# Scores by compressed and by selected keys in one matmul, and 32 units of attention in place of 48

## The chip, the cores and the metric

The kernel runs on one core of one Trainium2 chip. The metric is the device time of one execution in microseconds. The core has five engines with queues of their own: TensorE (PE in the profile; PEld is its weight load), VectorE (DVE), ScalarE (ACT), GpSimd (POOL) and SyncE (SP), which issues the transfers. TensorE multiplies a stationary 128-row operand with a moving one of up to 512 columns and writes into PSUM, eight banks of 512 columns each; DVE and ACT read them out.

## What is computed

One layer of a decoder for a prompt of 1024 tokens and eight single-token samples. The part that the change touches is the attention of the prompt, with eight heads in two groups of four, head width 64:

```python
def nsa_attend(q, gates, qpos, kc, vc, ksb, vsb, ovl, kw, vw, kwpos):
    s = einsum('bqghd,bcgd->bghqc', q, kc) * scale           # 63 compressed keys
    p_cmp = masked_softmax(s, c_end <= qpos)
    o_cmp = einsum('bghqc,bcgd->bqghd', p_cmp, vc)
    ...                                                       # top 16 of 16 blocks: all selected
    p = masked_softmax(q . kg * scale, kpos <= qpos)          # selected keys
    o_sel = p . vg
    p = masked_softmax(q . kw * scale, (dt >= 0) & (dt < 512))   # sliding window
    o_win = p . vw
    return gates[..., 0:1] * o_cmp + gates[..., 1:2] * o_sel + gates[..., 2:3] * o_win
```

Around it stand a norm with conditioning, one wide projection `z = h @ w_in`, a short gated convolution as a second branch, and three output projections.

## The kernel before

Values are kept in 32 bits, and each product is made of a high and a low half of its operands: a projection is three matmuls for each 128-deep slice (`Hh` by `wh`, `Hl` by `wh`, `Hh` by `wl`), a score two (`qh` and `ql`, lines 937 to 974). The attention runs after the key and value projections, over eight blocks of 128 queries.

**Units.** `unit(i, g, br)` (line 914) is the work of query block `i`, group `g` and branch `br`: 0 compressed (64 key columns), 1 selected (128 to 1024 columns, all blocks up to `i`), 2 window (128 to 640). Keys are cut into chunks of at most 512 columns by `chunks` (line 889). There are 48 units, in the order block, group, branch (line 1021).

**Two halves of a unit.** `a_steps` (line 937) goes over four heads `j`. For each chunk it makes two matmuls into a PSUM bank of tag `S` (three banks), then one pass on DVE that adds the mask, writes the scores to SBUF tile `P` and keeps their running minimum in `mx` (line 953; scores are negated). After a head's last chunk ACT takes the exponential with its sum (line 956). After the fourth head DVE makes reciprocals and multiplies in the gate (lines 960 to 962), and the weights are scaled: on DVE for three heads (line 969), on ACT for the last where rows are longer than 256 (line 967), on POOL for the compressed branch, one instruction for each head (line 971). `b_steps` (line 977) turns the weights, 128 keys at a time: four transposes on PE into a bank of tag `T` (two banks), a copy on ACT for the high half (`ph`), a subtraction on DVE for the low half (`pl`), and two matmuls with the values into the one bank of tag `O`, which collects all three branches of a block and group. For the compressed branch it is four transposes from 64 columns, one operand `pc` that holds both halves, and one matmul that opens bank `O`. After the window branch ACT and DVE write the result to `QO` (line 1017).

**Laying over each other.** The loop from line 1037 emits the first half of unit `n` with the second half of unit `n - LAG`, `LAG` being 2, alternating in proportion to their counts of steps. After each step `advance` (line 1028) emits some of the filler: 288 steps of three matmuls each from the projections of the convolution branch (`fill_gen`, line 883), paced by a listed time `est` for each unit, at least 4.0 us. `prep_q` (line 902) makes the halves of a block's queries on ACT, DVE and POOL before its first unit. Weights for the filler come by transfers on SP, are rounded on ACT and subtracted on POOL (`W.lo, W.hi = P, A`). The order of emission is a priority: a scheduler places the instructions in the queues when the program is built, by its own estimates of readiness, and each queue then runs in order. Tiles of one tag share a fixed number of buffers (`bufs`); `P0`, `P1` and `P2` have one each.

**Key tiles.** `make_keys` (line 604) writes the high and low half of the keys into `KS[b][g]`, 128 rows by 1024 columns (line 755); `kc` holds the compressed keys in the same form, 64 columns for each group. What the filler leaves, and the fourth part of the convolution, follow after the attention on the same engines.

Of the kernel before, what the change touches and what calls it, by code (L numbers as in the profile page):

```python
# [19 lines left out]
F32 = mybir.dt.float32  # L20
F32R = mybir.dt.float32r
# [64 lines left out]
def _build(ctx, tc, nc, I, O):  # L86
# [27 lines left out]
    def sub(eng, out, a, b):  # L114
        eng.tensor_tensor(out=out, in0=a, in1=b, op=OP.subtract)  # L115
# [636 lines left out]
    run(proj(q_evac(3)), {(1, 4): lambda: compress2(1)})  # L752
    xctx.close()
    kp = pool("kp", "right", att)
    KS = [[kp.tile([128, T], F32R, name=f"K{b}{g}") for g in range(2)] for b in range(2)]
# [130 lines left out]

    W.lo, W.hi = P, A

    def chunks(n):
        if n <= 512:  # L890
            return [n]
        return {640: [384, 256], 768: [512, 256], 896: [512, 384], 1024: [512, 512]}[n]

    class Unit:
        pass

# [12 lines left out]
            sub(P, QL[g][r], QO[r, :, qs], hh[g][r])  # L909
        QT[i] = hh  # L910

    WMAX = {0: 64, 1: 1024, 2: 640}

    def unit(i, g, br):
        u = Unit()
        u.i, u.g, u.br = i, g, br
        if br == 0:
            u.blocks, u.n = [0], 64
            u.ch = [(0, 64, cmsk[:, 56 - 8 * i:120 - 8 * i])]
        else:  # L920
            b0 = 0 if br == 1 else max(0, i - 4)
            u.blocks = list(range(b0, i + 1))
            u.n = 128 * len(u.blocks)
            edge = br == 2 and i >= 4
            u.ch, o = [], 0
            cl = chunks(u.n)
            for ci, n in enumerate(cl):
                m = msk[:, 128:128 + n]
                if ci == len(cl) - 1:
                    m = msk[:, 768 - n:768]  # L930
                elif ci == 0 and edge:
                    m = msk[:, 0:n]
                u.ch.append((o, n, m))
                o += n
        return u

    def a_steps(u):
        u.P = ap.tile([128, 4, WMAX[u.br]], F32, name=f"P{u.br}", tag=f"P{u.br}", bufs=1)
        u.mx = ap.tile([128, 4, 2], F32, name="mx", tag="mx", bufs=3)
        u.sm = ap.tile([128, 8], F32, name="sm", tag="sm", bufs=3)  # L940
        if u.br == 0:
            K = kc[:, u.g, :]
        else:
            K = KS[u.br - 1][u.g]
        k0 = u.blocks[0] * 128
        for j in range(4):
            hh = QT[u.i]
            for ci, (o, n, m) in enumerate(u.ch):
                ps = bank("S")
                mm(ps[:, :n], hh[u.g][:, j, :], K[:, k0 + o:k0 + o + n], True, False)  # L950
                mm(ps[:, :n], QL[u.g][:, j, :], K[:, k0 + o:k0 + o + n], False, True)
                init = 0.1 * BIG if ci == 0 else u.mx[:, j, ci - 1:ci]
                V.tensor_tensor_reduce(out=u.P[:, j, o:o + n], in0=ps[:, :n], in1=m, scale=1.0, scalar=init,  # L953
                                       op0=OP.add, op1=OP.min, accum_out=u.mx[:, j, ci:ci + 1])
                if ci == len(u.ch) - 1:
                    A.activation(u.P[:, j, 0:u.n], u.P[:, j, 0:u.n], AF.Exp, bias=u.mx[:, j, ci:ci + 1], scale=-1.0,  # L956
                                 accum_out=u.sm[:, j:j + 1])
                    if j == 3:
                        if u.br == 0:
                            V.tensor_scalar(u.sm[:, 0:4], u.sm[:, 0:4], 1e-30, None, op0=OP.max)  # L960
                        V.reciprocal(u.sm[:, 4:8], u.sm[:, 0:4])
                        V.tensor_tensor(out=u.sm[:, 4:8], in0=u.sm[:, 4:8],  # L962
                                        in1=gate[:, u.i, 12 * u.g + u.br:12 * u.g + u.br + 10:3], op=OP.mult)
                        for jj in range(4):
                            p = u.P[:, jj, 0:u.n]
                            if u.br > 0 and (jj == 3 and u.n > 256):
                                A.activation(p, p, AF.Copy, scale=u.sm[:, 4 + jj:5 + jj])
                            elif u.br > 0:
                                V.tensor_scalar(p, p, u.sm[:, 4 + jj:5 + jj], None, op0=OP.mult)  # L969
                            else:  # L970
                                P.tensor_tensor(out=p, in0=p, in1=u.sm[:, 4 + jj:5 + jj].to_broadcast([128, u.n]),
                                                op=OP.mult)
                yield max(0.2, 2 * n * 0.00042)

    OB = {}

    def b_steps(u):
        key = (u.i, u.g)
        if u.br == 0:
# [11 lines left out]
        pend = []  # L991

        def pv(kb, ph, pl, last):
            v = VS[u.br - 1]
            mm(OB[key], v[:, kb, u.g, :], pl, False, False)
            mm(OB[key], v[:, kb, u.g, :], ph, False, last)

        for n, kb in enumerate(u.blocks):
            pt = bank("T")
            for j in range(4):  # L1000
                PE.transpose(pt[:, j * 128:(j + 1) * 128], u.P[:, j, n * 128:(n + 1) * 128], ident)  # L1001
# [4 lines left out]
            pend.append((kb, ph, pl))  # L1006
            if len(pend) > 2:
                pv(*pend.pop(0), False)
            yield 0.87
# [12 lines left out]
    filler = fill_gen()  # L1022
    state = {"t": 0.0, "f": 0.0}
    est = lambda u: max(4.0, sum(2 * n * 0.00042 for _, n, _ in u.ch) * 4 + 0.87 * len(u.blocks))
    total = sum(est(u) for u in units)
    NFILL = 3 * 4 * 24

    def advance(dt):
        state["t"] += dt
        while filler and state["f"] < NFILL * min(1.0, state["t"] / total) - 1e-6:  # L1030
            state["f"] += 1
            next(filler, None)

    LAG = 2
    prep_q(0)
    done_q = 0
    for n in range(len(units) + LAG):
        la = []
        if n < len(units):
            u = units[n]  # L1040
            if u.i > done_q:
                prep_q(u.i)
                done_q = u.i
            la = a_steps(units[n])
        lb = b_steps(units[n - LAG]) if n >= LAG else iter(())

        na = 4 * len(units[n].ch) if n < len(units) else 0
        nb = len(units[n - LAG].blocks) + 1 if n >= LAG else 0
        ia = ib = 0
        share = est(units[min(n, len(units) - 1)]) / max(1, na + nb)  # L1050
        if n == len(units):
            share = 0
        while ia < na or ib < nb:
            if ib >= nb or (ia < na and ia * nb <= ib * na):
                next(la)
                ia += 1
            else:
                next(lb)
                ib += 1
            advance(share)  # L1060
        for _ in lb:
            pass
        for _ in la:
            pass
    for _ in filler:
        pass
# [362 lines left out]
```

## Time and profile before

| | us |
|---|---|
| median of 3 runs | 1097.35 |
| lowest and highest | 1094.35, 1097.61 |
| the profiled execution | 1093.98 |
| its span, first to last instruction | 1092.2 |
| PE busy | 1051.6 |
| DVE busy | 669.5 |
| ACT busy | 453.4 |
| POOL busy | 113.5 |

All rows come from the profiled execution; its span is 1.8 us shorter than its time. An instruction's busy time runs from its start to its end. On PE the end is modelled and matmuls overlap, so what a matmul costs is read from the distance to the start of the next. "Idle before" is time for which the engine stood still ahead of an instruction, with the engine and the output that released it. The attention stage lies from the first compressed score at 231.5 us to about 603 us; ahead of it are the norm, the projections of queries, keys and values and the compression, behind it projections that keep PE busy almost without a break.

### The profile page before, as it was taken

What the parts mean: (1) busy time and instruction counts of PE and PEld (TensorE: products, weight loads), DVE (VectorE), ACT (ScalarE), POOL (GpSimd) and SP (SyncE); (2) the same over time, 40 slices, a digit from 0 to 9 for tenths busy, and PEclk for the clock granted to TensorE, in tenths of its full rate; (3) what the DMA queues carried; (4) which work ended last, traced back from release to release, by engine and by line L of the source; (5) the groups of instructions that cost most, each with busy time, mean ns of one, the idle gap of its engine ahead of it and who ended that gap; (6) DMA issues with size and microseconds to landing.
All of it is one profiled execution on the core that took longest, in us unless ns stands there. A gap on an engine that the chain in (4) does not pass through costs nothing.

```text
span 1092.2 us, 17219 instructions
## 1 busy us (share of the span) xinstructions
PE 1051.6 (96%) x6406; PEld 967.0 (89%) x6406; DVE 669.5 (61%) x1789; ACT 453.4 (42%) x1006; POOL 113.5 (10%) x154
## 2 busy tenths in 40 slices
PE   5898999999999999999999999999999999999997
PEld 4688999988888899889888999999999999998785
DVE  4676656458987898879878734434455321584433
ACT  5566533356777777766666111111012111121221
POOL 3100000113222121211111010000000000020000
PEclk8899999989999999999999999999999999999999
DMA  9752242200000000000000412442232121332222
GB/s 324 212 147 75 77 101 59 76 23 21 19 20 21 20 20 20 20 20 9 13 20 23 116 40 69 131 148 69 76 75 53 39 59 39 99 114 79 78 78 77
DMA packets 103407, 75.97 MB, mean 70 GB/s; under 512 B 23873, under 2 KB 92680, under 8 KB 103324
## 3 DMA queue, kind: packets, MB, share of 16 engines
q1 hardware_dynamic: 103324, 74.88, 24.1%
q8 instruction: 50, 0.82, 0.3%
q14 instruction: 33, 0.27, 0.1%
HBM read 65.85 MB, written 9.01 MB: 69 GB/s over the span
## 4 chain that ended last, share of the span: by engine, by line
PE 79%; DVE 12%; ACT 4%; issue 1%; DMA 1%; SPq 0%; DVEq 0%; POOLq 0%; ACTq 0%; POOL 0%
PE psacc L106 47%; PE psS L106 18%; PE psO L106 6%; PE psT L1001 5%; DVE P L969 3%; DVE P L953 2%; ACT P L956 1%; DVE pl L115 1%; PE psT L106 1%; DVE pc L115 1%; DVE qh L112 1%; ACT xf L110 1%; DVE sm L962 1%; DVE QO L1017 1%; PE psT L357 1%
## 5 line engine op out<-in xcount | busy, mean ns | idle before, releaser
L106 PE MATMUL psacc<-Hh,wh 128*128 128x344 f32 x1072 | 356.6, 333 | 3.7 <-DVE Hh L112 3.7
L106 PE MATMUL psacc<-Hh,wl 128*128 128x344 f32 x1072 | 345.5, 323 | 1.0 <-DVE wl L115 1.0
L106 PE MATMUL psacc<-Hl,wh 128*128 128x344 f32 x1072 | 345.2, 322 | 0.0
L106 PEld LDWEIGHTS psacc<-Hh,wh 128*128 128x128 f32 x1072 | 203.2, 190 | 11.9 <-DVE Hh L112 4.2
L106 PEld LDWEIGHTS psacc<-Hl,wh 128*128 128x128 f32 x1072 | 203.1, 189 | 5.2 <-DVE Hl L115 0.5
L106 PEld LDWEIGHTS psacc<-Hh,wl 128*128 128x128 f32 x1072 | 203.0, 189 | 3.6 <-DVE wl L115 1.8
L956 ACT ACTIVATE P<-P,mx 128x64 f32<-128x64 f32 (+8 forms) x192 | 115.2, 601 | 48.5 <-DVE mx L953 47.8
L112 DVE CAST wh<-wraw 128x512 fp32r<-128x512 f32 x78 | 34.0, 442 | 121.0 <-PE psacc L106 114.5
L115 DVE TENSOR_TENSOR pl<-psT,ph 128x512 fp32r<-128x512 f32 x132 | 89.7, 687 | 26.7 <-ACT ph L110 26.1
L115 DVE TENSOR_TENSOR wl<-wraw,wh 128x512 fp32r<-128x512 f32 x112 | 76.5, 687 | 29.0 <-ACT wh L110 24.7
L110 ACT ACTIVATE ph<-psT 128x512 fp32r<-128x512 f32 x132 | 77.3, 590 | 36.9 <-PE psT L1001 36.5
L953 DVE CUSTOM_DVE_ANT_0 P<-psS,kbig 128x64 f32<-128x64 f32 (+4 forms) x192 | 81.3, 434 | 11.0 <-PE psS L106 9.9
L1001 PE MATMUL psT<-ident,P 128*128 128x128 f32 x528 | 82.6, 275 | 2.7 <-DVE mx L953 1.4
L1001 PEld LDWEIGHTS psT<-ident,P 128*128 128x128 f32 x528 | 63.6, 140 | 13.5 <-issue 3.3
L106 PE MATMUL psS<-K,qh 128*128 128x384 f32 (+3 forms) x192 | 66.2, 347 | 1.9 <-DVE mx L953 1.6
L115 POOL TENSOR_TENSOR wl<-wraw,wh 128x512 fp32r<-128x512 f32 x28 | 37.2, 1327 | 269.5 <-ACT wh L110 268.8
L106 PE MATMUL psS<-K,ql 128*128 128x384 f32 (+3 forms) x192 | 64.0, 335 | 0.0
L106 PE MATMUL psO<-pl,V 128*128 128x512 f32 x132 | 60.1, 456 | 1.0 <-DVE pl L115 0.9
L110 ACT ACTIVATE wh<-wraw 128x512 fp32r<-128x512 f32 x62 | 38.9, 628 | 41.6 <-PE psS L106 20.3
L106 PE MATMUL psO<-ph,V 128*128 128x512 f32 x132 | 52.1, 395 | 0.0
L969 DVE TENSOR_SCALAR P<-P,sm 128x640 f32<-128x640 f32 (+7 forms) x104 | 47.3, 513 | 0.7
L1220 ACT ACTIVATE M<-psacc 128x344 f32<-128x344 f32 x24 | 11.0, 457 | 87.8 <-PE psacc L106 87.8
(347 smaller groups left out, 1794.8 us busy)
## 6 DMA issues: line engine op xcount, KB each, us to landing
wraw<-w_in SPq DMA_DIRECT2D x76, 256.0 KB
x<-x_prompt SPq DMA_DIRECT2D x8, 512.0 KB
x<-w_ada SPq DMA_DIRECT2D x16, 256.0 KB
ar<-w_ada SPq DMA_DIRECT2D x16, 256.0 KB
wraw<-w_in SPq DMA_DIRECT2D x32, 128.0 KB
wraw<-w_cmp SPq DMA_DIRECT2D x16, 256.0 KB
wraw<-w_ada SPq DMA_DIRECT2D x16, 256.0 KB
wor<-w_out SPq DMA_DIRECT2D x16, 256.0 KB
```

Source lines behind the costliest of these rows:

```text
L106: PE.matmul(out, lhsT, rhs, start=start, stop=stop, skip_group_check=True)
L110: A.activation(out, in_, AF.Copy)
L112: eng.tensor_copy(out, in_)
L115: eng.tensor_tensor(out=out, in0=a, in1=b, op=OP.subtract)
L357: PE.matmul(ps[o:o + 32, :], cf[:, k, :], wraw.pop((b, k)), start=k < 4, stop=k >= 4, skip_group_check=True, tile_position=(0, o))
L953: V.tensor_tensor_reduce(out=u.P[:, j, o:o + n], in0=ps[:, :n], in1=m, scale=1.0, scalar=init, op0=OP.add, op1=OP.min, accum_out=u.mx[:, j ...
L956: A.activation(u.P[:, j, 0:u.n], u.P[:, j, 0:u.n], AF.Exp, bias=u.mx[:, j, ci:ci + 1], scale=-1.0, accum_out=u.sm[:, j:j + 1])
L962: V.tensor_tensor(out=u.sm[:, 4:8], in0=u.sm[:, 4:8], in1=gate[:, u.i, 12 * u.g + u.br:12 * u.g + u.br + 10:3], op=OP.mult)
L969: V.tensor_scalar(p, p, u.sm[:, 4 + jj:5 + jj], None, op0=OP.mult)
L1001: PE.transpose(pt[:, j * 128:(j + 1) * 128], u.P[:, j, n * 128:(n + 1) * 128], ident)
L1017: V.tensor_tensor(out=QO[r, :, 128 * u.i:128 * u.i + 128], in0=o[0:64].rearrange("p (j q) -> p j q", j=4), in1=tmp, op=OP.add)
L1220: A.activation(M[:, f, cs], acc, AF.Tanh, scale=0.5)
```

## The change

The compressed branch is no unit any more. The tile of the selected keys is widened by 64 columns in front, into which the compressed keys are copied, and the first chunk of a selected unit is scored together with them: one matmul over 64 + n columns, then two passes on DVE, one for each part, into `P0` and `P1` with minima and sums of their own. Chunks of selected keys are cut anew so that 64 more columns fit into a bank. POOL scales all four heads of the compressed weights in one instruction. The second half of a selected unit begins with the transposes of the compressed weights; their product with the values is emitted after the transposes of the first block of keys. There are 32 units. The second half of unit `n - 1` is laid beside the first half of unit `n`: steps of both get places on a line from 0 to 1 by listed times, the second half from `w` on, which stands for 2.5 us; the filler is emitted along the same line.

```diff
-            copy(A, KS[b][g][r, :], raw[r, 0:T])
-            sub(V, KS[b][g][o, :], raw[r, 0:T], KS[b][g][r, :])
+            ks = slice(KC[b], KC[b] + T)
+            copy(A, KS[b][g][r, ks], raw[r, 0:T])
+            sub(V, KS[b][g][o, ks], raw[r, 0:T], KS[b][g][r, ks])
...
+    KC = [64, 0]
+    KS = [[kp.tile([128, KC[b] + T], F32R, name=f"K{b}{g}") for g in range(2)] for b in range(2)]
+    for g in range(2):
+        copy(V, KS[0][g][:, 0:64], kc[:, g, :])
...
-        return {640: [384, 256], 768: [512, 256], 896: [512, 384], 1024: [512, 512]}[n]
+    CHUNKS = {1: {128: [128], 256: [256], 384: [384], 512: [256, 256], 640: [384, 256], 768: [384, 384],
+                  896: [448, 448], 1024: [384, 320, 320]},
+              2: {128: [128], 256: [256], 384: [384], 512: [512], 640: [384, 256]}}
...
+            subs = [(len(u.parts) - 1, o, n, m)]
+            k0 = KC[br - 1] + 128 * b0 + o
+            if ci == 0 and br == 1:
+                subs.insert(0, (0, 0, 64, cmsk[:, 56 - 8 * i:120 - 8 * i]))
+                k0 = 0
+            u.ch.append((k0, sum(x[2] for x in subs), subs))
...
+            for k0, nt, subs in u.ch:
                 ps = bank("S")
+                mm(ps[:, :nt], hh[u.g][:, j, :], K[:, k0:k0 + nt], True, False)
+                mm(ps[:, :nt], QL[u.g][:, j, :], K[:, k0:k0 + nt], False, True)
+                c0 = 0
+                for x, o, n, m in subs:
...
+                    V.tensor_tensor_reduce(out=Pb[:, j, o:o + n], in0=ps[:, c0:c0 + n], in1=m, scale=1.0, scalar=init,
+                                           op0=OP.add, op1=OP.min, accum_out=mx[:, j, ci % 2:ci % 2 + 1])
...
+                        if br == 0:
+                            P.tensor_tensor(out=Pb, in0=Pb, in1=sm[:, 4:8].rearrange("p (j o) -> p j o", o=1).to_broadcast(
+                                [128, 4, 64]), op=OP.mult)
+                            continue
...
+        if u.br == 1:
             OB[key] = bank("O")
             pt = bank("T")
             for j in range(4):
-                PE.transpose(pt[:64, j * 128:(j + 1) * 128], u.P[:, j, 0:64], ident)
+                PE.transpose(pt[:64, j * 128:(j + 1) * 128], u.P[0][:, j, :], ident)
             pc = ap.tile([128, 512], F32R, name="pc", tag="ph", bufs=3)
             copy(A, pc[0:64], pt[:64])
             sub(V, pc[64:128], pt[:64], pc[0:64])
-            yield 0.44
-            mm(OB[key], vc[:, u.g, :], pc, True, False)
-            yield 0.3
-            return
+            yield 0.45
...
             pend.append((kb, ph, pl))
+            if pc is not None:
+                mm(OB[key], vc[:, u.g, :], pc, True, False)
+                pc = None
...
-    units = [unit(i, g, br) for i in range(8) for g in range(2) for br in range(3)]
+    units = [unit(i, g, br) for i in range(8) for g in range(2) for br in (1, 2)]
...
+    def a_times(u):
+        return [max(0.22, 2 * nt * 0.00046) for _ in range(4) for _, nt, _ in u.ch]
+    def b_times(u):
+        return [0.45] * (u.br == 1) + [0.9] * len(u.blocks) + [0.5]
+    est = lambda u: max(5.0, sum(a_times(u)) + sum(b_times(u)))
+    WAIT = 2.5
...
-    LAG = 2
...
+        span = est(u) if u else sum(tb)
+        fill = span * 137.0 / total
+        w = min(0.7, WAIT / (span + fill)) if u else 0.0
+        ev, x = [], 0.0
+        for t in ta:
+            ev.append((x / sum(ta), 0, t))
+            x += t
+        x = 0.0
+        for t in tb:
+            ev.append((w + (1 - w) * x / sum(tb), 1, t))
+            x += t
+        ev.sort()
+        past = 0.0
+        for k, (at, which, t) in enumerate(ev):
+            if u:
+                advance(span * (at - past))
+                past = at
+            next(lb if which else la)
```

The sum `total` of `est` over the 32 units is 225.5 by these times.

## Rows read from the trace of the kernel before

**Rows 1.** The page's busy time, share of the span and instructions of two engines.
```profile
PE 1051.6 (96%) x6406; PEld 967.0 (89%) x6406; DVE 669.5 (61%) x1789; ACT 453.4 (42%) x1006; POOL 113.5 (10%) x154
```

**Rows 2.** The attention stage by windows; the first line names the columns.
```profile
core 0: us, PE busy (x) PEld busy (x) DVE busy (x) ACT busy (x) POOL busy (x), PEclk, DMA share, GB/s
231.50:603.00 371.50, 359.61 (x2257) 324.75 (x2258) 313.82 (x978) 258.86 (x627) 76.06 (x111) 0.99 0.08 19
```

**Rows 3.** PE groups in the stage: count, busy us, mean ns, idle us before, releaser.
```profile
L106 PE MATMUL psS<-kc,qh 128*128 128x64 f32 x64 | 14.0, 223 | 2.4 <-DVE mx L953 2.2 <-DVE qh L112 0.3
...
L106 PE MATMUL psO<-pc,vc 128*128 128x512 f32 x16 | 7.7, 478 | 4.0 <-DVE pc L115 3.8
```

**Rows 4.** PE in order of time (start us, duration us): 64 and 128 columns.
```profile
231.65 0.28 PE L106 MATMUL psS<-kc,ql 128*128 128x64 f32 x1
231.76 0.28 PE L106 MATMUL psS<-kc,qh 128*128 128x64 f32 x1
...
248.90 0.28 PE L106 MATMUL psS<-K,qh 128*128 128x128 f32 x1
249.01 0.27 PE L106 MATMUL psS<-K,ql 128*128 128x128 f32 x1
```

**Rows 5.** PE in order of time: 256, 512 and 384 columns.
```profile
446.11 0.28 PE L106 MATMUL psS<-K,ql 128*128 128x256 f32 x1
446.23 0.40 PE L106 MATMUL psS<-K,qh 128*128 128x512 f32 x1
446.46 0.39 PE L106 MATMUL psS<-K,ql 128*128 128x512 f32 x1
...
577.32 0.34 PE L106 MATMUL psS<-K,qh 128*128 128x384 f32 x1
577.49 0.34 PE L106 MATMUL psS<-K,ql 128*128 128x384 f32 x1
```

**Rows 6.** DVE groups in the stage: passes over scores by width.
```profile
L953 DVE CUSTOM_DVE_ANT_0 P<-psS,kbig 128x512 f32<-128x512 f32 x40 | 27.3, 685 | 4.7 <-PE psS L106 4.4
L953 DVE CUSTOM_DVE_ANT_0 P<-psS,kbig,mx 128x256 f32<-128x256 f32 x48 | 22.8, 479 | 3.8 <-PE psS L106 3.0
L953 DVE DVE_READ_ACCUMULATOR2_ANT mx<- 128x1 f32 x256 | 21.0, 82 | 0.0
...
L953 DVE CUSTOM_DVE_ANT_0 P<-psS,kbig 128x256 f32<-128x256 f32 x16 | 6.4, 416 | 0.5 <-PE psS L106 0.5
```

**Rows 7.** Groups from 225 to 605 us: exponential, scalings, GpSimd's work, reciprocal.
```profile
L956 ACT ACTIVATE P<-P,mx 128x640 f32<-128x640 f32 x40 | 33.0, 826 | 15.2 <-DVE mx L953 15.0
L115 POOL TENSOR_TENSOR wl<-wraw,wh 128x512 fp32r<-128x512 f32 x23 | 30.8, 1338 | 91.7 <-ACT wh L110 91.0 <-PE psacc L106 0.6
...
L971 POOL TENSOR_TENSOR P<-P,sm 128x64 f32<-128x64 f32 x64 | 16.9, 295 | 71.0 <-DVE sm L962 53.2 <-ACT ph L110 7.7 <-DVE u L852 6.7
L969 DVE TENSOR_SCALAR P<-P,sm 128x640 f32<-128x640 f32 x30 | 14.8, 548 | 0.2
...
L961 DVE RECIPROCAL sm<-sm 128x4 f32<-128x4 f32 x48 | 8.4, 175 | 4.3 <-ACT P L956 3.5
```

**Rows 8.** The gate multiplication by its line: duration ns min/median/max, first and last start.
```profile
L962 DVE TENSOR_TENSOR sm<-sm,gate x48: 151/163/1244, 235.5 to 588.9; 128x4 f32<-128x4 f32 x48
```

**Rows 9.** POOL and DVE in order of time (start us, duration us).
```profile
515.38 1.30 POOL L115 TENSOR_TENSOR wl<-wraw,wh 128x512 fp32r<-128x512 f32 x1 [15.05 <-ACT wh L110]
...
515.60 1.10 DVE L962 TENSOR_TENSOR sm<-sm,gate 128x4 f32<-128x4 f32 x1
```

**Rows 10.** PE in order of time: the two halves of one score chunk.
```profile
442.76 0.40 PE L106 MATMUL psS<-K,qh 128*128 128x512 f32 x1
...
443.82 0.48 PE L106 MATMUL psS<-K,ql 128*128 128x512 f32 x1
```

**Rows 11.** Weight loads' waits in the stage: us in total, times, longest us.
```profile
PEld psT L1001 <- DVE P L969: 0.3, 1, 0.3
```

More of the change, by code (lines that the diff above doesn't have):

```diff
@@ L916, in unit @@
         u.i, u.g, u.br = i, g, br
[L917 to L934, printed above, removed]
+        b0 = 0 if br == 1 else max(0, i - 4)
@@ new lines, in unit @@
+        u.blocks = list(range(b0, i + 1))
+        u.n = 128 * len(u.blocks)
+        u.parts = [(0, 64)] if br == 1 else []
+        u.parts.append((br, u.n))
+        edge = br == 2 and i >= 4
+        u.ch, o = [], 0
+        cl = CHUNKS[br][u.n]
+        for ci, n in enumerate(cl):
+            m = msk[:, 128:128 + n]
+            if ci == len(cl) - 1:
+                m = msk[:, 768 - n:768]
+            elif ci == 0 and edge:
+                m = msk[:, 0:n]
+            subs = [(len(u.parts) - 1, o, n, m)]
[4 more added lines that the diff above has]
+            u.ch.append((k0, sum(x[2] for x in subs), subs))
+            o += n
@@ L935, in unit @@
         return u
     def a_steps(u):
[L938 to L945, printed above, removed]
+        u.P, u.mx, u.sm = {}, [], []
+        for br, n in u.parts:
+            u.P[br] = ap.tile([128, 4, (64, 1024, 640)[br]], F32, name=f"P{br}", tag=f"P{br}", bufs=1)
+            u.mx.append(ap.tile([128, 4, 2], F32, name="mx", tag="mx", bufs=3))
+            u.sm.append(ap.tile([128, 8], F32, name="sm", tag="sm", bufs=3))
@@ L946, in a_steps @@
+        K = KS[u.br - 1][u.g]
+        hh = QT[u.i]
         for j in range(4):
-            hh = QT[u.i]
-            for ci, (o, n, m) in enumerate(u.ch):
+            seen = [0] * len(u.parts)
+            for k0, nt, subs in u.ch:
                 ps = bank("S")
[L950 to L963, printed above, removed]
-                        for jj in range(4):
[L965 to L969, printed above, removed]
-                            else:
-                                P.tensor_tensor(out=p, in0=p, in1=u.sm[:, 4 + jj:5 + jj].to_broadcast([128, u.n]),
-                                                op=OP.mult)
-                yield max(0.2, 2 * n * 0.00042)
@@ new lines, in a_steps @@
+                mm(ps[:, :nt], hh[u.g][:, j, :], K[:, k0:k0 + nt], True, False)
+                mm(ps[:, :nt], QL[u.g][:, j, :], K[:, k0:k0 + nt], False, True)
+                c0 = 0
+                for x, o, n, m in subs:
+                    (br, total_n), mx, sm = u.parts[x], u.mx[x], u.sm[x]
+                    Pb, ci = u.P[br], seen[x]
+                    init = 0.1 * BIG if ci == 0 else mx[:, j, (ci - 1) % 2:(ci - 1) % 2 + 1]
+                    V.tensor_tensor_reduce(out=Pb[:, j, o:o + n], in0=ps[:, c0:c0 + n], in1=m, scale=1.0, scalar=init,
+                                           op0=OP.add, op1=OP.min, accum_out=mx[:, j, ci % 2:ci % 2 + 1])
+                    seen[x] += 1
+                    c0 += n
+                    if o + n == total_n:
+                        A.activation(Pb[:, j, 0:total_n], Pb[:, j, 0:total_n], AF.Exp, bias=mx[:, j, ci % 2:ci % 2 + 1], scale=-1.0,
+                                     accum_out=sm[:, j:j + 1])
@@ new lines, in a_steps @@
+                if j == 3 and (k0, nt, subs) == u.ch[-1]:
+                    for x, (br, n) in enumerate(u.parts):
+                        sm, Pb = u.sm[x], u.P[br]
+                        if br == 0:
+                            V.tensor_scalar(sm[:, 0:4], sm[:, 0:4], 1e-30, None, op0=OP.max)
+                        V.reciprocal(sm[:, 4:8], sm[:, 0:4])
+                        V.tensor_tensor(out=sm[:, 4:8], in0=sm[:, 4:8],
+                                        in1=gate[:, u.i, 12 * u.g + br:12 * u.g + br + 10:3], op=OP.mult)
+                        if br == 0:
+                            P.tensor_tensor(out=Pb, in0=Pb, in1=sm[:, 4:8].rearrange("p (j o) -> p j o", o=1).to_broadcast(
+                                [128, 4, 64]), op=OP.mult)
+                            continue
+                        for jj in range(4):
+                            p = Pb[:, jj, 0:n]
+                            if jj == 3 and n > 256:
+                                A.activation(p, p, AF.Copy, scale=sm[:, 4 + jj:5 + jj])
+                            else:
+                                V.tensor_scalar(p, p, sm[:, 4 + jj:5 + jj], None, op0=OP.mult)
@@ L975, in _build @@
+                yield max(0.22, 2 * nt * 0.00046)
     OB = {}
@@ L1000, in b_steps @@
             for j in range(4):
-                PE.transpose(pt[:, j * 128:(j + 1) * 128], u.P[:, j, n * 128:(n + 1) * 128], ident)
+                PE.transpose(pt[:, j * 128:(j + 1) * 128], u.P[u.br][:, j, n * 128:(n + 1) * 128], ident)
             ph = ap.tile([128, 512], F32R, name="ph", tag="ph", bufs=3)
@@ L1019, in b_steps @@
         yield 0.43
-    units = [unit(i, g, br) for i in range(8) for g in range(2) for br in range(3)]
+    units = [unit(i, g, br) for i in range(8) for g in range(2) for br in (1, 2)]
     filler = fill_gen()
     state = {"t": 0.0, "f": 0.0}
-    est = lambda u: max(4.0, sum(2 * n * 0.00042 for _, n, _ in u.ch) * 4 + 0.87 * len(u.blocks))
+    NFILL = 3 * 4 * 24
+    def a_times(u):
+        return [max(0.22, 2 * nt * 0.00046) for _ in range(4) for _, nt, _ in u.ch]
+    def b_times(u):
+        return [0.45] * (u.br == 1) + [0.9] * len(u.blocks) + [0.5]
@@ L1025, in _build @@
+    est = lambda u: max(5.0, sum(a_times(u)) + sum(b_times(u)))
     total = sum(est(u) for u in units)
-    NFILL = 3 * 4 * 24
+    WAIT = 2.5
     def advance(dt):
         state["t"] += dt
-        while filler and state["f"] < NFILL * min(1.0, state["t"] / total) - 1e-6:
+        while state["f"] < NFILL * min(1.0, state["t"] / total) - 1e-6:
             state["f"] += 1
             next(filler, None)
-    LAG = 2
     prep_q(0)
[L1036 to L1060, printed above, removed]
@@ new lines, in _build @@
+    for n in range(len(units) + 1):
+        u = units[n] if n < len(units) else None
+        v = units[n - 1] if n else None
+        if u and u.i > (v.i if v else 0):
+            prep_q(u.i)
+        la, ta = (a_steps(u), a_times(u)) if u else (iter(()), [])
+        lb, tb = (b_steps(v), b_times(v)) if v else (iter(()), [])
+        span = est(u) if u else sum(tb)
[16 more added lines that the diff above has]
+            next(lb if which else la)
+        if u:
+            advance(span * (1 - past))
+        for _ in la:
+            pass
@@ L1061, in _build @@
         for _ in lb:
-            pass
-        for _ in la:
             pass
```

11 lines of the change are left out of this document (3 added, 8 removed).

## The prediction, before the result was known

> **What bounds the kernel now.** I read the page first: TensorE (PE) is busy almost the whole span and VectorE (DVE) 61% of it [rows 1]. That share is a mean over stages, so the next view is the stage that the diff touches, the attention from 231.5 to 603.0 us of the trace. There PE is busy 359.6 of 371.5 us and DVE 313.8 [rows 2]. So 11.9 us of PE time are visibly idle, and DVE, at 84%, is close behind: PE work sets the pace, and nearly every hole in PE is DVE being late. The waits of PE say so: a score matmul waiting for a PSUM bank that DVE has to read out, and the product with the compressed values waiting for the subtraction that makes its operand [rows 3]. What the stage is made of is read from the times at which matmuls start one after the other, not from their durations, which overlap. Back to back and at the full clock, a score matmul of 64 columns takes 0.11 us, one of 128 columns also 0.11 [rows 4], one of 256 columns 0.12, of 512 columns 0.23 and of 384 columns 0.17 [rows 5]. So below 256 columns a matmul costs a floor of 0.11 us whatever its width, and this is what the change goes at.
>
> **The matmuls taken away.** Eight query blocks, two groups, four heads, two matmuls (high and low half of the query): 128 matmuls of 64 columns go. At 0.11 us each that is 14.1 us of PE time [rows 4]. They lie on the path wherever PE has other work in hand, which is 97% of the stage.
>
> The Trainium skill ("TensorE: Matmul & The Clock Gate", section "Back-to-back issue gap") gives columns divided by 2.4 GHz plus 2.5 ns, 29 ns for 64 columns; by it the removal would be worth 3.7 us and the columns added below 3.4, so nothing would be gained. The trace does not bear that out: 110 ns stand between these starts [rows 4].
>
> **The columns added.** The 64 compressed keys now ride in the first chunk of the selected keys. By straight lines between the widths of [rows 4, 5], 192 columns cost 0.11 to 0.12, 320 columns 0.145 and 448 columns 0.20. Old against new chunks, one matmul for each: block 0 gains 0 to 0.01; 256 to 320, +0.025; 384 to 448, +0.03; 512 to 320 and 256, +0.035; blocks 4 to 7, +0.03, +0.02, +0.03 and +0.03. That is 0.20 us for a row of eight blocks, times 16 matmuls (2 groups, 4 heads, 2 halves): +3.2 us. Ends: +2.5 and +4.
>
> **DVE work added.** The number of passes over compressed scores is as before; the selected keys of block 3 go from one pass to two, and of block 7 from two to three: 16 passes more. A 512-column pass takes 685 ns, a 256-column one 416 (first) or 479 (later), and each ends in an 82 ns read of its accumulator [rows 6]. So 512 in one is 0.77 us and 256 twice 1.06: +0.29 us each, 4.6 us in all. DVE is 84% busy and its lateness is what stops PE, so part of this shows: between 0 and 4.6 I take a third, +1.5 us.
>
> **Waits that go.** PE stood idle 4.0 us ahead of the product with the compressed values and 2.4 us ahead of the compressed scores [rows 3]. The first moves behind the transposes of the next block, so its operand has some 0.4 us longer; I count 3 us gone. The second goes with its instruction, but the bank that it waited for is then waited for by the next score chunk; I count 1 us. Together -4 us (ends 0 and -6.4).
>
> **The distance between scores and weighted sums.** Before, a unit's transposes come two units after its scores; after, one. What lies between is a chain: the last pass over scores (0.48 and 0.08), the exponential (0.83), reciprocal and gate (0.17 and 0.16), three scalings on DVE at 0.55: 3.4 us for a window unit [rows 6 to 8]. The new loop emits 2.5 us divided by (own time plus filler) of the unit ahead of the first transpose. For a window unit of 640 keys the listed times sum to 7.4, filler adds 7.4 x 137/225.5 = 4.5, the fraction is 0.21, and of the 2.4 us of scores and 4.5 of filler 1.4 us stand ahead. So some 2 us of chain are uncovered at each of 31 boundaries: 62 us if the queues followed the emission order, nothing if other matmuls are drawn in. They are not in that order now: the two halves of one score chunk, emitted next to each other, stand 1.06 us apart with other matmuls between them [rows 10], so the scheduler fills holes by its own times, and the filler projection (matmuls that wait for no softmax; the new loop reckons them at 137 us) is there to be drawn on. The row of before is 0.3 us of waiting on these scalings in the whole stage, at distance two [rows 11]. I take +2 us; ends 0 and +62. Behind a late transpose PE's whole queue stands, as it runs in order, and with it ScalarE's copies and DVE's subtractions.
>
> **GpSimd.** It scaled 64 pieces of 64 columns at 295 ns, 18.9 us; now 16 pieces of 256 columns. A line through 295 ns at 64 and 1338 ns at 512 columns [rows 7] gives 0.74 us, 11.9 in all. GpSimd is off the path, but this scaling now sits right ahead of a unit's first transposes. And it can hold DVE: a gate multiplication of four columns, 163 ns in the median, took 1.10 us while GpSimd ran a subtraction from 515.38 to 516.68, and ended at 516.70 [rows 8, 9].
>
> The Trainium skill ("SBUF — State Buffer", section "SBUF: two separate sides") has the rule: the two engines share a port pair under an exclusive lock, and the loser blocks for the whole instruction. The trace agrees. By it the new 0.74 us scaling stands against the second gate multiplication right behind it on DVE, up to 16 x 0.74 = 12 us of DVE time.
>
> In my sum this is inside the +2 above. The copies of the compressed keys into the key tiles (two small DVE instructions) and the two narrow tile columns cost under 1 us beside projection matmuls that do not wait for DVE; counted at nothing, 0.5 us if that cover is gone. No DMA moves.
>
> **Sum.** -14.1 + 3.2 + 1.5 - 4 + 2 = -11.4 us, of a profiled execution of 1094.0 us (span 1092.2): 1082.6. The median of the runs shown, 1097.35, is 3.4 us above that execution, so on the scale of the median 1086.
>
> **The rivals.** (1) The late weights: the chain above is not filled. It decides from the point at which the mean hole at a boundary exceeds 13.4/31 = 0.43 us (13.4 being the sum without its +2). For it: 2 us uncovered, GpSimd in the chain, DVE held by GpSimd. Against: 137 us of filler, and reordering in the trace. At 0.8 us for each boundary, 25 us: 1097.4 - 13.4 + 25 = 1109. (2) DVE becomes the bound: it would need 318 of 360 us; what PE saves comes back as waits for score banks. Then the 10.9 net us of PE are hardly seen: 1094 to 1100, say 1097. Against it: DVE still has 42 us free and its share differs little between units now that a long selected unit is laid beside a short window unit and the other way round. (3) The better laying gives more: all 11.9 us of visible idle go, -14.1 + 3.2 + 1.5 - 11.9 = -21.3: 1076. For it: the idle stands at the compressed units, which are short in PE and long in latency and which vanish as units.
>
> The Trainium skill ("Perfetto Trace Analysis", section "Identifying the Most-Contended Engine") would have weight loads read instead of matmul busy time; they fill 324.8 of 371.5 us [rows 2], so by it 47 us could be had, and rival 3 would go deeper.
>
> (4) The scheduler lays things as it likes, and only the merged matmuls count: -14.1 + 3.2 + 1.5 = -9.4, 1088, within the forecast.
>
> **How the numbers follow.** Forecast with (4), 1080 to 1093: 0.47. Rival 3, 1068 to 1080: 0.19. Rival 2: 0.13. Rival 1: 0.21. Two runs of this kernel differ by some 0.3%, 3.3 us, so faster means under 1094.1 and slower over 1100.6. Faster 0.47 + 0.19 = 0.66, same 0.13, slower 0.21. The range goes from 1072 to 1108: it holds the forecast, rival 2, most of 3 and the milder half of 1.
>
> **What would show it.** Right: no 64-column score matmuls, a stage about 11 us shorter, PE still over 96% busy in it, transposes waiting for the scalings on DVE and GpSimd some 2 us in all. Wrong towards rival 1: PE's waits list transposes behind DVE or GpSimd scalings, tens of microseconds, several 1 us or longer. Towards 2: DVE over 92% busy in the stage and score matmuls waiting for the passes by over 10 us. Towards 3: under 4 us of idle PE. My forecast falls if small matmuls are not bound by their floor where they stand between others.

## The result, and the profile after

| | before, us | after, us |
|---|---|---|
| median | 1095.85 (4 runs) | 1087.71 (4 runs) |
| lowest and highest | 1094.22, 1097.61 | 1086.64, 1088.35 |
| the profiled execution, its span | 1093.98, 1092.2 | 1087.87, 1086.1 |

The ratio is 0.9929, with a 95% interval of 0.9912 to 0.9946: 8.1 us faster by the medians. By the interval the gain lies between 5.9 and 9.6 us. The forecast was 1086, a gain of 11.4 us, so the direction and the range held and the gain came out at seven tenths of the forecast. That the time itself came within 1.7 us of the forecast is in part luck: the forecast was reckoned from 1097.35, and the kernel before came out 1.5 us lower with a fourth run.

The page of the changed kernel, and its attention stage by windows: the first 13 us, the stretch to 300 us, and the whole stage, which ends at 596 us with the last attention result (columns: length, then busy time and instructions of PE, PEld, DVE, ACT, POOL, then PE's granted clock, DMA share, GB/s).

```profile
PE 1043.6 (96%) x6310; PEld 959.7 (88%) x6310; DVE 673.4 (62%) x1823; ACT 453.4 (42%) x1006; POOL 105.3 (10%) x106
```

```profile
231.00:244.10 13.10, 10.79 (x44) 9.32 (x45) 10.82 (x57) 7.06 (x31) 3.28 (x3) 0.61 0.01 1
244.10:300.00 55.90, 51.41 (x316) 47.12 (x315) 48.94 (x188) 39.02 (x124) 13.02 (x12) 0.97 0.08 20
...
231.10:596.00 364.90, 350.84 (x2153) 315.58 (x2154) 318.42 (x1010) 259.07 (x627) 68.25 (x63) 0.98 0.08 19
```

Against [rows 2] PE's instructions fall by 104: 128 matmuls of 64 columns go, the narrower chunks of blocks 3 and 7 bring 32 back, and 8 of the filler lie behind the stage now. PE's busy time falls by 8.8 us, and the stage from 371.5 to 364.9 us, 6.6 us where 11 were forecast. Idle PE has not fallen: 364.9 - 350.8 = 14.1 us, where it was 11.9. Of these, 6.8 us lie in the first 69 us. What PE waits for in the stage (us in total, times, longest us):

```profile
PE psT L1014 <- DVE P L987: 5.1, 9, 1.1
PE psO L106 <- DVE pc L115: 3.1, 2, 2.1
PE psT L1000 <- POOL P L979: 2.3, 4, 0.9
PE psS L106 <- DVE YB L872: 1.7, 1, 1.7
PE psO L106 <- DVE pl L115: 0.8, 1, 0.8
PE psS L106 <- DVE mx L963: 0.4, 1, 0.4
```

Of the waits of [rows 3] the one for `pc` is nearly as long as it was, 3.1 us in place of 3.8. Score matmuls wait 0.4 us for a pass on DVE (`mx`) and once 1.7 us more, put down to the filler's `YB` on DVE: there, at 232 us, the three pairs of scores before had filled the three banks, and DVE read the first of them at 233.1 us. Transposes now wait 5.1 us for the scaling on DVE (L987) and 2.3 us for the one on GpSimd (L979); before, PE itself waited for neither, its weight loads 0.3 us for DVE's [rows 11]. How the widened matmuls start, in order of time (start us, duration us):

```profile
231.42 0.28 PE L106 MATMUL psS<-K,qh 128*128 128x192 f32 x1
231.53 0.27 PE L106 MATMUL psS<-K,ql 128*128 128x192 f32 x1
...
258.59 0.31 PE L106 MATMUL psS<-K,qh 128*128 128x320 f32 x1
258.73 0.31 PE L106 MATMUL psS<-K,ql 128*128 128x320 f32 x1
...
441.43 0.37 PE L106 MATMUL psS<-K,qh 128*128 128x448 f32 x1
441.63 0.37 PE L106 MATMUL psS<-K,ql 128*128 128x448 f32 x1
```

192 columns take 0.11 us, 320 take 0.14 and 448 take 0.20, as the straight lines through [rows 4, 5] had it.

### The profile page after: what moved, and what is told of

Read it like the earlier page. It is cut to its first block, busy times and chain, and to the rows that moved or that the text cites. A ratio compares the mean times of both kernels' runs of the same rounds, so it can differ in the third digit from the quotient of the medians.

```text
span 1086.1 us, 17011 instructions
## 1 busy us (share of the span) xinstructions
PE 1043.6 (96%) x6310; PEld 959.7 (88%) x6310; DVE 673.4 (62%) x1823; ACT 453.4 (42%) x1006; POOL 105.3 (10%) x106
## 4 chain that ended last, share of the span: by engine, by line
PE 60%; DVE 2%; ACT 0%; issue 0%; DVEq 0%; POOLq 0%; ACTq 0%
PE psacc L106 38%; PE psS L106 13%; PE psO L106 4%; PE psT L1014 3%; PE psT L106 1%; DVE P L987 1%; DVE P L963 0%; DVE pl L115 0%; PE psT L1205 0%; PE psT L1000 0%; DVE YB L867 0%; DVE qh L112 0%; DVE sm L976 0%; DVE QO L1033 0%; ACT ph L110 0%
## 5 line engine op out<-in xcount | busy, mean ns | idle before, releaser
L968 ACT ACTIVATE P<-P,mx 128x64 f32<-128x64 f32 (+5 forms) x192 | 115.1, 601 | 41.6 <-DVE mx L963 40.4
L1014 PE MATMUL psT<-ident,P 128*128 128x128 f32 x528 | 87.6, 278 | 5.5 <-DVE P L987 5.1
L963 DVE CUSTOM_DVE_ANT_0 P<-psS,kbig 128x64 f32<-128x64 f32 (+4 forms) x192 | 74.2, 409 | 11.7 <-PE psS L106 10.8
L106 PE MATMUL psS<-K,qh 128*128 128x384 f32 (+6 forms) x208 | 69.5, 335 | 2.4 <-DVE YB L872 1.7
L106 PE MATMUL psS<-K,ql 128*128 128x384 f32 (+6 forms) x208 | 69.2, 333 | 0.0
L987 DVE TENSOR_SCALAR P<-P,sm 128x640 f32<-128x640 f32 (+7 forms) x104 | 53.3, 567 | 0.4
```

The costliest lines, as they stand in the source:

```text
L106: PE.matmul(out, lhsT, rhs, start=start, stop=stop, skip_group_check=True)
L963: V.tensor_tensor_reduce(out=Pb[:, j, o:o + n], in0=ps[:, c0:c0 + n], in1=m, scale=1.0, scalar=init, op0=OP.add, op1=OP.min, accum_out=mx[ ...
L968: A.activation(Pb[:, j, 0:total_n], Pb[:, j, 0:total_n], AF.Exp, bias=mx[:, j, ci % 2:ci % 2 + 1], scale=-1.0, accum_out=sm[:, j:j + 1])
L987: V.tensor_scalar(p, p, sm[:, 4 + jj:5 + jj], None, op0=OP.mult)
L1014: PE.transpose(pt[:, j * 128:(j + 1) * 128], u.P[u.br][:, j, n * 128:(n + 1) * 128], ident)
```

## The experiments

All were timed in five rounds beside the kernel before. A ratio is to that kernel; what counts is its distance from 0.9929, the changed kernel's, which was timed once, with four runs. The kernel before took 1093 to 1096 us in the different sittings, so gains are reckoned from ratios; between two runs they are uncertain by 2 to 3 us.

**The matmuls alone.** The changed kernel with the compressed columns scored apart again:

```diff
-                mm(ps[:, :nt], hh[u.g][:, j, :], K[:, k0:k0 + nt], True, False)
-                mm(ps[:, :nt], QL[u.g][:, j, :], K[:, k0:k0 + nt], False, True)
+                for s0, s1 in (((0, 64), (64, nt)) if len(subs) == 2 else ((0, nt),)):
+                    mm(ps[:, s0:s1], hh[u.g][:, j, :], K[:, k0 + s0:k0 + s1], True, False)
+                    mm(ps[:, s0:s1], QL[u.g][:, j, :], K[:, k0 + s0:k0 + s1], False, True)
```

> The changed kernel, but the 64 compressed columns are scored by a pair of matmuls of their own again, into the same bank and within the same step, so that order, passes on DVE and laying are as in the changed kernel and only PE's work is as before: 128 matmuls of 0.11 us more, 2.9 to 3.2 us of columns less. Theory (the merge carries the gain, PE work is on the path): 1087.7 + 10.9 = 1098.6 us, 1.002 to 1.004 of the kernel before, since the new laying then loses 2 to 3 us against the old. Rival (the new laying carries it and the matmuls were hidden): 1088 to 1091 us, under 0.996.

Measured: 1096.41 us, ratio 1.0009 (0.9996 to 1.0022). The merge is worth 0.80%, 8.7 us (6.4 to 11.1 with both intervals), all of the gain. The new laying with the 128 matmuls back is as slow as the old laying: between 0.4 us faster and 2.4 slower.

**The same in query blocks 0 to 3 alone.** The condition gets `and u.i < 4`.

> The changed kernel with the compressed columns scored by matmuls of their own again, but in query blocks 0 to 3 alone: half of the 128 matmuls come back, 5.5 us of PE work with the columns taken off. Theory (in the short early units PE is not what is late, so the merge gains nothing there): 1087 to 1089 us, 0.992 to 0.994 of the kernel before. Rival (the merge gains evenly, 8.7 us over eight blocks): 1091 to 1093 us, 0.996 to 0.998.

Measured: 1088.44 us, ratio 0.9945 (0.9929 to 0.9961). Of the 8.7 us the early half brings 0.16%, 1.7 us, which the intervals can't tell from nothing (-0.8 to 4.3), and the late half 1.0009 - 0.9945 = 0.64%, 7.0 us.

The profiled executions show the same, cut where the result of block 3 is written. Early and late half of the changed kernel, then the early half of this run, then the late half of the run with all the matmuls apart:

```profile
231.10:369.40 138.30, 129.18 (x770) 115.98 (x771) 121.14 (x438) 101.45 (x296) 32.15 (x30) 0.95 0.07 18
369.40:596.00 226.60, 221.66 (x1385) 199.60 (x1384) 197.28 (x573) 157.63 (x332) 36.10 (x33) 1.00 0.08 20
```

```profile
231.20:369.40 138.20, 130.73 (x835) 119.44 (x836) 119.61 (x439) 102.38 (x296) 31.87 (x30) 0.98 0.07 18
```

```profile
371.90:605.50 233.60, 226.79 (x1439) 205.53 (x1438) 199.05 (x568) 157.60 (x329) 35.70 (x32) 1.00 0.08 19
```

Late, the merge takes 5.1 us off PE's busy time (226.8 to 221.7) and 1.9 us off its idle time (6.8 to 4.9), 7.0 us together. Early, it takes 1.6 us off the busy time (130.7 to 129.2) and adds as much idle time (7.5 to 9.1), so nothing is gained. The granted clock there is 0.95 against 0.98, so a part of what the merge saves goes into slower matmuls. How far the lower clock belongs to the change is not shown: two of the changed kernel's four executions have a mean clock of 0.990 and 0.991, like those of this run (0.988 to 0.990).

**DVE time.** Forty passes more, each cut out of a longer one:

```diff
...
+            if br == 2 and u.n >= 512 and ci == 0:
+                h = n // 2
+                subs = [(0, o, h, m[:, 0:h]), (0, o + h, h, m[:, h:n])]
...
```

> The changed kernel, with the first DVE pass over a window unit's scores cut in two halves for units of 512 and 640 keys: 40 passes more at about 0.27 us (0.19 of fixed time and 0.08 of reading the accumulator), 11 us of DVE time, no matmul and no other work changed. Theory (a third of added DVE time shows, as in the forecast): 1090 to 1092 us. Rival (DVE at 87% of the stage is the bound now): 1096 to 1099 us. Rival (hidden): 1087 to 1089 us.

Measured: 1087.58 us, ratio 0.9920 (0.9900 to 0.9939): nothing to be seen. The DVE groups of its stage show that the passes are there (192 columns twice, where 384 took 550 ns), each with its read of the accumulator, 312 of them in place of the changed kernel's 272; then its stage by windows, and two instructions in order of time:

```profile
L967 DVE DVE_READ_ACCUMULATOR2_ANT mx<- 128x1 f32 x312 | 25.7, 82 | 0.0
...
L967 DVE CUSTOM_DVE_ANT_0 P<-psS,kbig,mx 128x192 f32<-128x192 f32 x32 | 13.2, 412 | 0.2
...
L967 DVE CUSTOM_DVE_ANT_0 P<-psS,kbig 128x192 f32<-128x192 f32 x32 | 11.2, 353 | 3.4 <-PE psS L106 3.0
```

```profile
231.80:597.10 365.30, 350.63 (x2157) 316.78 (x2158) 323.58 (x1090) 258.79 (x627) 67.70 (x63) 0.98 0.08 19
```

```profile
428.51 0.35 DVE L967 CUSTOM_DVE_ANT_0 P<-psS,kbig 128x192 f32<-128x192 f32 x1
428.78 0.08 DVE L967 DVE_READ_ACCUMULATOR2_ANT mx<- 128x1 f32 x1
```

By their durations the passes would add 353 + 412 + 82 - 550 = 297 ns each, 11.9 us in all. But DVE's instructions overlap, the read starts 0.27 us after a pass of 0.35 us, and DVE's busy time rises by 5.2 us only (318.4 to 323.6), 0.13 us for each pass. The time came out 1.0 us under the changed kernel's, with 2.8 us to either side. So 5.2 us more on DVE do not all appear, and DVE's total, at 318 of 365 us, is no bound; whether a third of them appears the run can't tell. That the waits of PE name DVE must have another reason than its total.

**Emission earlier and later.** `WAIT` at 0 and at 5:

> The changed kernel with WAIT 0 in place of 2.5: the second half of a unit is emitted from the very start of the next unit's first half. Theory (the chain from scores to scaled weights is too short covered and the emission order matters): waits of transposes on the scalings of DVE and GpSimd grow from 7.4 us to 12 or more, 1091 to 1098 us. Rival (the scheduler lays by its own estimates, emission is only a tie break): 1086 to 1089 us and the same waits.

> The changed kernel with WAIT 5.0 in place of 2.5. Theory (late weights cost 7 us of idle PE): the waits on scalings fall to 4 us or less and the time to 1083 to 1086 us. Rival (what is pushed back crowds the end of the unit and DVE's queue): waits move to the subtractions and the banks, 1088 to 1092 us.

Measured: 1090.03 us, ratio 0.9944 (0.9925 to 0.9963), and 1086.46 us, ratio 0.9911 (0.9892 to 0.9930). Each overlaps the interval of 2.5, so the times alone settle neither; the order 0, 2.5, 5 is the one expected, over 3.6 us, and both times lie just outside the ranges of the theory. The waits of PE in the stage do settle where it comes from. At 0:

```profile
PE psT L1014 <- DVE P L987: 7.5, 13, 1.1
PE psT L1000 <- POOL P L979: 7.1, 13, 1.6
```

and at 5:

```profile
PE psO L106 <- DVE pl L115: 4.8, 6, 1.7
PE psT L1000 <- POOL P L979: 2.3, 3, 1.1
...
PE psT L1014 <- DVE P L987: 0.5, 1, 0.5
```

The waits on scalings are 14.6, 7.4 and 2.8 us: emission order does reach the queues, and the chain from scores to scaled weights is covered too short. At 5 the waits come back in another place, as its rival had it: those for the subtraction `pl` are 4.8 us, where they were 0.8, and all waits of PE listed in the stage are 13.2 us, where they were 13.7.

**More filler for short units.** `est` at least 8.0 in place of 5.0:

> The changed kernel with a least listed time of 8.0 us for a unit in place of 5.0, so that the short units of query blocks 0 to 3 get more of the filler and the long ones less. Theory (the merge gains nothing in blocks 0 to 3, because PE lacks work there, waits, and its clock falls to half for 13.7 us in place of 6.8): the low clock shortens to 7 us or less, 1082 to 1086 us. Rival (filler missing at the end of the stage costs as much): 1087 to 1092 us.

Measured: 1086.83 us, ratio 0.9925 (0.9904 to 0.9946), no change. The first 14 us, of this kernel and then of the changed one (columns as above):

```profile
231.00:245.00 14.00, 10.96 (x58) 9.97 (x57) 9.35 (x54) 7.67 (x33) 2.24 (x3) 0.76 0.01 1
```

```profile
231.00:245.00 14.00, 11.69 (x51) 10.22 (x51) 11.04 (x58) 7.92 (x36) 3.28 (x3) 0.63 0.01 1
```

The granted clock rose there from 0.63 to 0.76, and the time did not follow: PE's waits behind GpSimd's scaling went from 2.3 to 7.2 us. The rise is no work of this edit: the kernels with the matmuls apart and with `WAIT` at 0 have 0.76 there too. The time is the rival's, but its reason, filler missing at the end of the stage, was not looked at. More matmuls for the early units did not help.

**Scalings to ACT.** `jj >= 2` in place of `jj == 3`:

> The changed kernel with the weights of two heads in place of one scaled on ACT where rows are longer than 256: 24 scalings of some 0.6 us leave DVE, 24 of 0.6 to 1.15 us come to ACT. Theory (the chain ahead of the transposes is what costs, not DVE's total): the chain is a scaling shorter on DVE, waits behind DVE's scaling fall from 5.1 to 3 us, 1084 to 1087 us. Rival (ACT's copies come later and PE waits for those): 1088 to 1092 us.

Measured: 1091.09 us, ratio 0.9968 (0.9955 to 0.9980), slower by 0.39%, 4.3 us. My theory fell: the waits behind DVE's scaling were 5.8 us, not fewer than 5.1, and weight loads waited 6.5 us for `pl`, where it was 4.8. ACT, at 71% of the stage in the changed kernel, is in the same chain, between transposes and subtraction; that its later copies cost the time is argued from there, not tried.

**The compressed weights scaled on DVE.** `V.tensor_tensor` in place of `P.tensor_tensor`:

> The changed kernel with the scaling of the compressed weights on DVE in place of GpSimd (16 instructions of 256 columns, 0.64 us each there). Theory (GpSimd's queue and its hold on DVE delay the first transposes of a selected unit; DVE time itself was hidden in the run with 40 more passes): the 2.3 us of waits behind GpSimd's scaling go, 1084 to 1087 us. Rival (the chain on DVE gets longer by the same time, the waits move to DVE's scaling): 1087 to 1089 us.

Measured: 1085.23 us, ratio 0.9916 (0.9898 to 0.9935). It leans the way of the theory by 1.4 us, inside the intervals. The waits moved as the rival had it: PE waits 7.9 us for scalings, 6.1 for L987 and 1.8 for the one moved to DVE, where it was 7.4.

**GpSimd's subtractions of weights moved to DVE.** One line ahead of the units, in the changed kernel and in the kernel before:

```diff
-    W.lo, W.hi = P, A
+    W.lo, W.hi = V, A
```

> The changed kernel with the low halves of the filler's weights subtracted on DVE (0.69 us each) in place of GpSimd (1.30 us each) during the attention: 23 instructions move. Theory (GpSimd's two-input instructions hold DVE for up to 1.3 us at a time, while 11 us of added DVE time were hidden): DVE's scalings and gate multiplications lose their long cases, waits fall, 1083 to 1087 us. Rival (16 us more on DVE is over what is hidden, or the weights come later): 1088 to 1096 us.

> The kernel before, with the low halves of the filler's weights subtracted on DVE in place of GpSimd during the attention, as the run on the changed kernel had it, which gained 7 us there. Theory (GpSimd's hold on DVE costs most where the softmax chain is one unit from its transposes, that is with the new laying): 2 to 5 us faster than the kernel before, 0.995 to 0.998. Rival (the hold costs the same in either laying): 7 us, 0.993 to 0.994. Rival (with 48 units the longer DVE queue is felt): no gain or a loss.

Measured: on the changed kernel 1079.75 us, ratio 0.9863 (0.9844 to 0.9883), 0.66% or 7.2 us under the changed kernel, more than the theory's range. On the kernel before 1091.37 us, ratio 0.9972 (0.9959 to 0.9985), 0.28% or 3.1 us. The stage of the first:

```profile
231.50:588.10 356.60, 346.41 (x2157) 313.71 (x2158) 324.32 (x1034) 257.93 (x627) 38.57 (x40) 0.99 0.08 20
```

The moved subtractions are 23 of 0.69 us, 16 us by their durations, yet DVE's busy time rises by 5.9 us only (318.4 to 324.3): part of the rest is what its other instructions no longer lose beside GpSimd (gate products 160 ns in the mean for 199, scalings of 384 columns 524 for 689). GpSimd's own queue is not the reason: the waits of PE behind its scaling stay, 2.7 us for 2.3, while those behind DVE's fall from 5.1 to 2.6. So what had made DVE late was in good part GpSimd beside it, and by these times the new laying pays more for that than the old.

**All of it together.** Weights subtracted on DVE, compressed weights scaled on DVE, `WAIT = 5.0`; and then the queries' low halves on DVE too (`sub(V, QL[g][r], ...)` in `prep_q`):

> The changed kernel with three edits of the runs so far: filler's weights subtracted on DVE, compressed weights scaled on DVE, WAIT 5.0. Theory (they take away different waits: the hold, GpSimd's queue in the chain, the short cover): 1075 to 1079 us, 0.982 to 0.985. Rival (they take away the same waits, or 26 us more on DVE is felt): 1079 to 1083 us.

> As the run with all three edits, and the low halves of the queries subtracted on DVE too (16 instructions of 1.35 us leave GpSimd, which then has the gated convolution's products alone). Theory (the long cases of the query casts on DVE, beside those subtractions, go): 1 to 3 us under the run with three edits. Rival (11 us more on DVE at 92% are felt): 0 to 4 us over it.

Measured: 1073.64 us, ratio 0.9806 (0.9790 to 0.9821), and 1070.27 us, ratio 0.9782 (0.9767 to 0.9798), both a little below the ranges of their theories. The last is the fastest kernel here, 24 us under the kernel before and 16 under the changed one. Its stage, and what PE still waits for in it:

```profile
230.80:578.10 347.30, 341.82 (x2157) 312.74 (x2158) 322.66 (x1065) 256.65 (x627) 8.39 (x9) 1.00 0.08 20
```

```profile
PE psT L1000 <- ACT P L968: 1.5, 1, 1.5
PE psO L106 <- DVE pl L115: 1.4, 2, 0.7
PE psS L106 <- DVE mx L963: 1.1, 1, 1.1
PE psO L106 <- DVE pc L115: 0.9, 3, 0.3
```

DVE is busy 93% of the stage and PE idles 5.5 us; PE waits for no scaling, and the clock of this execution is granted in full through the stage.

**How GpSimd holds DVE.** The same DVE instructions in the changed kernel (duration: the second number behind the bar, mean ns)

```profile
L963 DVE CUSTOM_DVE_ANT_0 P<-psS,kbig 128x384 f32<-128x384 f32 x72 | 39.4, 551 | 5.0 <-PE psS L106 4.7
...
L112 DVE CAST qh<-QO 64x512 fp32r<-64x512 f32 x15 | 10.6, 706 | 0.8 <-PE psS L106 0.3
L976 DVE TENSOR_TENSOR sm<-sm,gate 128x4 f32<-128x4 f32 x48 | 9.1, 199 | 0.9
...
L987 DVE TENSOR_SCALAR P<-P,sm 128x384 f32<-128x384 f32 x12 | 7.7, 689 | 0.0
...
L987 DVE TENSOR_SCALAR P<-P,sm 128x128 f32<-128x128 f32 x16 | 6.1, 442 | 0.1
```

and in the last kernel, whose GpSimd works 8 us in the stage in place of 68:

```profile
L963 DVE CUSTOM_DVE_ANT_0 P<-psS,kbig 128x384 f32<-128x384 f32 x72 | 39.0, 549 | 1.3 <-PE psS L106 1.3
...
L976 DVE TENSOR_TENSOR sm<-sm,gate 128x4 f32<-128x4 f32 x48 | 7.2, 156 | 0.2
...
L112 DVE CAST qh<-QO 64x512 fp32r<-64x512 f32 x15 | 6.3, 422 | 0.5
...
L987 DVE TENSOR_SCALAR P<-P,sm 128x384 f32<-128x384 f32 x12 | 4.4, 414 | 0.0
...
L987 DVE TENSOR_SCALAR P<-P,sm 128x128 f32<-128x128 f32 x16 | 3.5, 278 | 0.0
```

The means of casts, scalings and gate products, which work from SBUF to SBUF, are longer by up to two thirds in the kernel with more GpSimd work; the pass that reads its scores from PSUM is not, 551 against 549 ns. Not every instruction within SBUF is held: the reciprocal of four columns has a mean of 171 ns in both. The Trainium skill ("SBUF — State Buffer", section "SBUF: two separate sides") puts it as an exclusive lock on a port pair that DVE takes for two-input SBUF work and for its faster SBUF modes; these two fences agree.

One case in full, from the changed kernel in order of time (the last line from PE's own rows):

```profile
249.11 1.56 DVE L987 TENSOR_SCALAR P<-P,sm 128x128 f32<-128x128 f32 x2
249.11 1.28 POOL L115 TENSOR_TENSOR wl<-wraw,wh 128x512 fp32r<-128x512 f32 x1 [0.20 <-ACT wh L110]
...
251.57 0.40 ACT L968 ACTIVATE P<-P,mx 128x128 f32<-128x128 f32 x1 [2.53 <-DVE mx L963]
...
252.47 0.59 ACT L110 ACTIVATE pc<-psT 64x512 fp32r<-64x512 f32 x1
...
253.09 0.68 DVE L115 TENSOR_TENSOR pc<-psT,pc 64x512 fp32r<-64x512 f32 x1 [1.41 <-ACT pc L110]
```

```profile
253.83 0.50 PE L106 MATMUL psO<-pc,vc 128*128 128x512 f32 x1 [2.07 <-DVE pc L115]
```

Two scalings of 0.28 us take 1.56 us while GpSimd subtracts weights: GpSimd is done at 250.39, the second scaling 0.28 us later. DVE's next passes come late, so ACT's exponentials do, ACT's copy of `pc` stands behind them in its queue, DVE's subtraction behind that copy, and PE stands 2.07 us. Of the scalings' time on that path half a microsecond was their own, and one more was GpSimd's; the rest of the 2.07 us is the chain behind them.

## Why the prediction was right in direction and too high in size

- **The merged matmuls, -14.1 + 3.2 = -10.9: measured -8.7.** The floor of 0.11 us and the widened matmuls came as reckoned, and the intervals of the sum (6.4 to 11.1) just hold 10.9. What they do not allow is its early half: in blocks 0 to 3 the removal pays 1.7 us, at most 4.3, where the same working gives 5.4; in blocks 4 to 7 it pays 7.0, where it gives 5.3 (half of 14.1, less 1.8 for the columns). The step that failed is "they lie on the path wherever PE has other work in hand, which is 97% of the stage": the share was a mean, and early PE also waits for the chain of DVE and ACT. That the early half pays little is shown by the run with the early matmuls put back; the reasons are read from one profiled execution of each, as much more idle PE as busy time was saved, and a lower granted clock, and were not tried apart. The late half's surplus over its matmuls, 1.9 us less idle PE in the profiles, is inside the intervals. The formula of the Trainium skill that the prediction sets against its rows ("TensorE: Matmul & The Clock Gate", section "Back-to-back issue gap") is, by that section, for an isolated matmul, and counts too little at small widths where each matmul comes with a weight load, as here; so the 110 ns do not speak against the page.
- **DVE's added passes, +1.5: too dear.** The 4.6 us behind it add up durations, which overlap on DVE. At the 0.13 us for each that the run with forty passes shows, sixteen are about 2.1 us, an estimate, and that run saw no slowing from two and a half times as many. PE's waits name DVE because DVE is late at places, not because it is full.
- **Waits that go, -4: partly; the distance, +2: there and too small.** The product with `pc` waits 3.1 us in place of 3.8, where 3 us were to go: its later place did not cover the chain to its operand. Score matmuls wait 2.1 us in place of 3.8, the 1.7 behind `YB` included. Together that is 2.4 us less. Transposes wait 7.4 us for scalings, mechanism and place as the first rival had them, at 0.24 us for each of 31 boundaries, under the 0.43 from which it would have decided. All in all idle PE rose by 2.2 us, where these two terms had it fall by 2. The laying as a whole cost 1.0 us (interval -0.4 to 2.4), where these terms with DVE's gave -0.5, so the times hardly show these errors; the waits do.
- **GpSimd, "inside the +2": the largest thing missed.** [rows 8, 9] showed the hold, and the forecast counted only what the change's own scaling would add. The subtraction of the weights on GpSimd alone costs the changed kernel 7 us against the same work on DVE. The merged scaling took 0.64 us (0.74 forecast); moving it to DVE gave 1.4 us, inside the intervals.
- **The rivals.** The late weights are real but smaller than the gain; DVE as the bound fell; the better laying gave nothing by itself; the merge alone, 1088 by the fourth, is what happened, because the laying came out even. That its number is so near is luck in part: its sum of -9.4 holds 1.5 us for DVE of which no run shows a trace, and a merge larger than the one measured.

## What to carry to other kernels

Merging small matmuls paid at the floor price of each (0.11 us here) or better in the half of the stage where PE was nearly always busy, and hardly in the other; a mean over the stage hides that. When an engine is named in the waits but added work on it is hidden, look at what stretches its instructions: the same instruction compared with and without GpSimd beside it told more here than any busy share. And durations that overlap do not add up: what forty passes cost was read from DVE's busy time, at less than half of their sum. The holds cost more with the new laying, 7.2 us against 3.1; that the shorter distance between a softmax and its use is the reason was not tried by itself.

## What was not expected of the hardware

A GpSimd instruction of 1.3 us can stretch a DVE instruction from SBUF to SBUF from 0.16 us to 1.10 [rows 8, 9] and leave one that reads PSUM as it is (551 and 549 ns), so 68 us of GpSimd work, slower for each element than DVE (1.30 against 0.68 us for the same subtraction), cost more than giving most of it to a DVE already busy 87% of the stage. And PE's clock fell to its lower level, 1.2 GHz, in the first units of the changed kernel's profiled execution (granted 0.63 over 14 us), after PE had stood 1.7 us behind DVE:

```profile
233.70 0.36 PE L106 MATMUL psS<-K,qh 128*128 128x192 f32 x1 [1.68 <-DVE YB L872]
```

In the profiled execution of the last kernel it was granted in full through the stage. That is one execution: the mean clock over the whole of its other four was 0.986 to 0.988, where this one had 0.994, so that GpSimd's work makes the clock fall is not shown.
